# The first pair of w_ffn_in blocks as plain products instead of Strassen-type products

## The chip, the cores and the metric

The kernel runs on one core of one Trainium2 chip. The metric is the device time of one execution in microseconds (us). The kernel before has a median of 2129.55 us over 3 runs (2124.32 to 2131.04).

## The reference

An encoder of two layers works on 1024 tokens of width 1024. In each layer a mixer (a Fourier group, windowed attention, memory attention) is followed by a SwiGLU block, and both are normed on the way in and out:

```
x = x + RMSNorm_post(mixer(RMSNorm_pre(x)))
h = RMSNorm_pre_ffn(x)
gate, up = split(h @ w_ffn_in)            # 1024 x 1024 times 1024 x 5632
x = x + RMSNorm_post_ffn((silu(gate) * up) @ w_ffn_out)
```

The change lies in `h @ w_ffn_in`, in both layers, and there in the first 256 columns of gate and of up.

## The kernel before, in words

All matrix products are in float32r, a rounded form of float32, in three passes: each operand is split into a rounded high part (a cast on ScalarE, ACT, line 151) and the rest (a subtraction on VectorE, DVE, or on GpSimd, POOL, line 152), and high x high, high x low and low x high are summed in PSUM. TensorE (PE) does the products. The tile framework puts in the waits and orders each engine's instructions by its own schedule, in which the order of the code is the priority; so the order on an engine can differ from that of the code. Each engine then works through its instructions in order.

**The quads.** `w_ffn_in` is worked in 11 pairs, p = 0 to 10, each of a gate quad and an up quad (`Quad`, line 1067). A quad covers 256 columns, 1024 input channels and 1024 tokens as 2 x 2 blocks and needs seven products of half blocks instead of eight (a Strassen scheme). `ORDER` (line 1065) is 2, 4, 5, 1, 6, 7, 3. One product is 12 matmuls of 128 x 128 on 512 tokens, so a quad has 84. For a product, `weights` (line 1083) adds or subtracts two weight blocks where it needs a sum (five of seven; line 1093, DVE) and splits the result. `step` (line 1111) runs the product and combines the results with copies (line 1108, ACT) and sums on DVE and POOL (lines 1123 to 1139). `gate_out` (1142) takes Silu of the four gate blocks, `up_out` (1150) multiplies and writes seven sums of them to `actd` in DRAM, from where `ffn_out` takes them.

**The token blocks.** The right hand sides are made once per layer by `Blocks` (line 1016). `tile` (1024) transposes one tile of 128 tokens on PE (line 1032, eight transposes into two PSUM tiles `hTp`) and copies it raw to SBUF on ACT (1033). Raw blocks are named by token half and channel half: b11 and b21 for tokens 0 to 511, b12 and b22 for the others. `sum(i, c)` (1035) makes a quarter of the split right hand side of product i: 2 is b11, 5 is b22, 4, 1 and 6 are sums of two blocks (line 1050; the one of 6 on POOL), and 7 and 3 are b21 and b12 after `last` (1058) has changed them (1062 on POOL, 1063 on DVE). Products 2 and 4 need the first token half alone, the others need all eight tiles.

**The passage from mixer to w_ffn_in.** The loop `for i in range(NT + 4)` (line 1345) skews four steps: attention scores and values of tile i (with `out_prep`, which splits and squares the attention result), `out` of tile i-2 (the mixer's last products, `mo`, whose columns are combined at line 1007, then norm, residual and norm, lines 318, 325 and 281, 289), `tile` of i-4, and loads for tile i-1. From i = 8 on the block sums and the first products are put in between: blocks 2, then the gate quad's load, blocks 4 and its product 2 at i = 9, and at i = 10 the up quad's load and the rest of products 2 and 4. Blocks 5, 1 and 6 follow as their tiles come.

**Space.** SBUF is laid out by hand in two arenas with numbered places; small rings give out places in turn: `qws` for raw quad weights, `wcs` for split weights, `wsums` and `sums` for sums, `acts`, `silus` and `sns` for outputs. `HB` (line 1019) says where each split block lies. PSUM has four tags of two buffers each, `sc`, `pT`, `av` and `pd`.

Of the kernel before, what the change touches and what calls it, by code (L numbers as in the profile page):

```python
# [19 lines left out]
P = 128  # L20
# [48 lines left out]
def tile_encoder(ctx: ExitStack, tc: tile.TileContext, T, C, out):  # L69
# [58 lines left out]
    ems, es_ring, y1s = run(16, 4, 2), run(33, 5, 3), run(6, 2, 1)  # L128
    sqs, pms, xfs = run(16, 2, 2), run(20, 2, 2), Ring(16, 20, 24, 28, 32, 0)
    qws, sns, silus, acts = Ring(32, 0, 16, 20), Ring(36, 38, 40, 42, 32, 34), run(8, 5, 2), run(18, 7, 2)  # L130
    sums, wsums = run(8, 4, 2), Ring(4, 6)
    ras, rbs, bsums, xs_ = run(40, 3, 2), run(46, 6, 2), Ring(58, 32, 34), Ring(36, 24)

    zzs, dhs, tabs = run(112, 2, 4), run(64, 2, 4), run(72, 4, 2)
    mps, phs, yys = run(24, 2, 4), run(16, 3, 4), run(104, 2, 4)
    wcs, abs_ = Ring(112, 116, 96, 100, 48, 52, 56, 60), Ring(80)

    def sm(n, name="v"):
        if name not in smp:
# [876 lines left out]
    class Blocks:  # L1016


        HB = {2: (64, 72), 4: (80, 88), 5: (16, 24), 1: (0, 8), 6: (32, 40), 7: (None, None), 3: (None, 104)}

        def __init__(self):
            self.raw, self.b = {}, {}

        def tile(self, h, t):
            half, c = divmod(t, 4)
            for kg in range(2):
                if c == 0:
                    self.raw[half, kg] = big(4, 512, dt=F32)
                pt = ps([4, P], "hTp", "pT")
                for j in range(4):  # L1030
                    k = kg * 4 + j
                    nc.tensor.transpose(pt[:, j, :], h[:, k * P : (k + 1) * P], ident)
                nc.scalar.copy(self.raw[half, kg][:, :, c * P : c * P + P], pt)

        def sum(self, i, c, lo_eng=None):

            b11, b21 = self.raw[0, 0], self.raw[0, 1]
            if i not in (2, 4):
                b12, b22 = self.raw[1, 0], self.raw[1, 1]
            sl = slice(c * P, c * P + P)  # L1040
            if i not in self.b:
                self.b[i] = [big(4, 512) if k is None else at(k, 4, 512, dt=F32R) for k in self.HB[i]]
            if i == 2:
                s = b11[:, :, sl]
            if i == 5:
                s = b22[:, :, sl]
            if i in (1, 4, 6):
                s = sums(4, P)
                x, y, op = (b21, b11, ALU.subtract) if i == 4 else (b11, b22 if i == 1 else b12, ALU.add)
                (nc.gpsimd if i == 6 else nc.vector).tensor_tensor(out=s, in0=x[:, :, sl], in1=y[:, :, sl], op=op)  # L1050
            if i == 7:
                s = b21[:, :, sl]
            if i == 3:
                s = b12[:, :, sl]
            hi, lo = (b[:, :, sl] for b in self.b[i])
            split(hi, lo, s, lo_eng)

# [9 lines left out]
    class Quad:  # L1067
# [6 lines left out]
        def load(self):  # L1074
            self.raw = []
            for kg in range(2):
                r = qws(4, 2, P)
                nc.sync.dma_start(
                    r, self.w[kg * 512 : kg * 512 + 512, self.c0 : self.c0 + 256].rearrange("(k p) (j c) -> p k j c", p=P, c=P)
                )  # L1080
                self.raw.append(r)

        def weights(self, i):
            a11, a12 = (r[:, :, 0] for r in self.raw)
# [64 lines left out]

    def up_out(q, g, actd, p):  # L1150

        V, G = nc.vector, nc.gpsimd
        a = [acts(512) for _ in range(4)]
        for i, c in enumerate(q.out):
            (G if i in (0, 3) else V).tensor_tensor(out=a[i], in0=c, in1=g[i], op=ALU.mult)  # L1155
        a11, a21, a12, a22 = a

        def put(i, s):
            nc.sync.dma_start(actd[i - 1, p], s)

        put(3, a11)
        put(4, a22)
        for i, x, y, eng in ((1, a11, a22, G), (2, a21, a22, V), (5, a11, a12, G)):
            s = acts(512)
            eng.tensor_tensor(out=s, in0=x, in1=y, op=ALU.add)
            put(i, s)
        V.tensor_tensor(out=a21, in0=a11, in1=a21, op=ALU.subtract)
        put(6, a21)
        G.tensor_tensor(out=a12, in0=a12, in1=a22, op=ALU.subtract)
        put(7, a12)  # L1170
# [1 line left out]
    def quads(l, p, hb):  # L1172
        return [Quad(l, j * DFF + 2 * p * P, hb) for j in range(2)]

    def ffn_in(l, hb, actd, first):

        for p in range(NFF // 2):
            gq, uq = quads(l, p, hb) if p else first
            order = ORDER if p else ORDER[2:]
            for q in (gq, uq):  # L1180
                if p:
                    q.load()
                for i in order:
                    q.step(i)
                if q is gq:
                    g = gate_out(gq)
            up_out(uq, g, actd, p)
            if p == 0:
                qws.ks, wsums.ks = (44, 48, 52, 56), (4, 6, 0, 2)

# [132 lines left out]
    for l in range(DEPTH):  # L1323
        mix.zf(1, 2)
        mix.kvz_load()
        kvz = mix.skewed(mix.kvz, mix.kvz_turn, NT)
        weave(mix.fourier_units(), kvz[:8] + [mix.q_load] + kvz[8:])
        q = mix.skewed(mix.q, mix.q_turn, NT)
        for u in q[:4]:
            u()  # L1330
        mem.load()
        weave(mix.mem_units(), q[4:8] + [mix.fm_load] + q[8:])
        fm = mix.fm_units(pmd)
        weave(mix.att_units(0), fm[:6] + [mix.out_load] + fm[6:])
        mix.out_gains()
        xs = x_in if l == 0 else x2d
        hb = Blocks()
        hs = {}
        first = gq, uq = quads(l, 0, hb)
        qws.ks, wsums.ks = (32, 0, 16, 20), (4, 6)  # L1340
        for r in (qws, wsums, xfs, sns, silus, acts, sums, wcs):
            r.i = 0
        mix.values_32()
        att = mix.att_units(1)
        for i in range(NT + 4):
            if i < NT + SKEW:
                att[i]()
            if 2 <= i < NT + 2:
                hs[i - 2] = mix.out(i - 2, x1d[i - 2])
            if i >= 4:  # L1350
                hb.tile(hs.pop(i - 4), i - 4)
            if 1 <= i < NT + 1:
                mix.out_rows(i - 1, xs[i - 1], pmd[i - 1])
            if i == NT:
                for c in range(4):
                    hb.sum(2, c)
            if i == NT + 1:
                gq.load()
                for c in range(4):
                    hb.sum(4, c)  # L1360
                gq.step(2)
            if i == NT + 2:
                uq.load()
                gq.step(4)
                uq.step(2)
                uq.step(4)
            if i >= NT:
                for n in (5, 1):
                    hb.sum(n, i - NT)
            if i > NT:  # L1370
                for c in (i - NT - 1,) if i < NT + 3 else (2, 3):
                    hb.sum(6, c)
                    hb.last(c)
        for n in (7, 3):
            for c in range(4):
                hb.sum(n, c)
        ffn_in(l, hb, actd, first)

        junks.ks = (6,)
        nhT = [None, None]  # L1380
        st = {}
        if l + 1 < DEPTH:
            mem = Memory(l + 1, 16, 0, 16, 28, "pT")
            mix = Mix(l + 1, nhT, mem)

        xt = {}

        def last_x(t):
            xt[t] = xs_(D)
            nc.sync.dma_start(xt[t], x1d[t])  # L1390

        def last_tile(t, f):
            if t == 0:
# [12 lines left out]

        last = l + 1 == DEPTH
        abs_.i = 0
        abs_.ks = (64, 72, 80, 88, 16, 24, 0, 8, 32, 40, 48, 56, 96, 104, 112) if last else (80, 88, 48, 56, 96, 104)

        def after(i):
            if last:
                return
            if i == 5:
                mem.make()
            if i == 1:
                mix.zf_load()
# [49 lines left out]
```

## Time and profile before

The profile shows one execution of the kernel. In a row of a group, after the bar, stand busy us, mean ns of one, and the idle time before it with what ended it. A timeline row has start, length, engine, line, operation, names, count, and in brackets the idle time before it and what released it. A row of stretches gives for each engine busy time and, in brackets, the number of instructions.

| What | Value |
|---|---|
| Median of 3 runs | 2129.55 us |
| The profiled execution's own time | 2127.03 us |
| Its span, first to last instruction | 2125.2 us |
| PE busy with matmuls | 2008.2 us (94%) |
| DVE busy | 1594.6 us (75%) |
| ACT busy | 1068.3 us (50%) |
| POOL busy | 862.9 us (41%) |
| Mean granted TensorE clock | 0.974 |

### The profile page before, as it was taken

How to read it: one execution, taken by the hardware profiler on the slowest of the kernel's cores; microseconds unless marked ns; L12 is line 12 of the kernel's file. 1: busy time of each engine (PE TensorE's matmuls, PEld its weight loads, DVE VectorE, ACT ScalarE, POOL GpSimd, SP SyncE). 2: the span in 40 equal slices, each digit the busy share in tenths (PEclk: the TensorE clock that was granted, in tenths of full speed). 3: DMA queues.
4: the chain of work that ended last, by engine and by line, in shares of the span. 5: the costliest groups of instructions: out<-in, count | busy, mean ns of one | idle time of the engine just before them, and what ended most of it. 6: DMA issues, size and time to landing. Idle time of an engine off the chain costs nothing. (4 is left out here: it accounts for less than half of the span.)

```text
span 2125.2 us, 28513 instructions
## 1 busy us (share of the span) xinstructions
PE 2008.2 (94%) x9586; PEld 1655.2 (78%) x9586; DVE 1594.6 (75%) x2445; ACT 1068.3 (50%) x2269; POOL 862.9 (41%) x858
## 2 busy tenths in 40 slices
PE   7998999699999999999899979997999999989997
PEld 6886787488888887888778868775888888877885
DVE  7568666998877877667967686669887877877674
ACT  6477767553333334444545676775333333345441
POOL 4234437643423434321544444576443423432222
PEclk9999999899999999999999989998999999999998
DMA  6112122422332326987721122142332332389872
GB/s 222 45 50 65 65 95 106 152 65 95 122 100 94 111 95 193 352 270 263 257 84 45 49 70 99 67 143 95 104 109 95 119 100 93 119 290 328 278 229 79
DMA packets 173603, 287.52 MB, mean 135 GB/s; under 512 B 15480, under 2 KB 73360, under 8 KB 173456
## 3 DMA queue, kind: packets, MB, share of 16 engines
q1 hardware_dynamic: 165392, 266.82, 37.9%
q10 hardware_dynamic: 8064, 18.88, 2.3%
q8 instruction: 75, 1.23, 0.2%
q14 instruction: 72, 0.59, 0.1%
HBM read 219.06 MB, written 66.58 MB: 134 GB/s over the span
## 5 line engine op out<-in xcount | busy, mean ns | idle before, releaser
L151 ACT CAST arena_r<-arena_f 128x512 fp32r<-128x512 f32 (+1 forms) x780 | 444.6, 592 | 679.8 <-PE qz L1103 116.4
L152 DVE TENSOR_TENSOR arena_r<-arena_f,arena_r 128x512 fp32r<-128x512 f32 x676 | 545.2, 829 | 173.8 <-ACT arena_r L151 170.2
L1234 PE MATMUL fo<-arena_r 128*128 128x512 f32 x1848 | 437.5, 398 | 28.4 <-ACT arena_r L151 15.2
L1234 PEld LDWEIGHTS fo<-arena_r 128*128 128x128 f32 x1848 | 354.1, 193 | 106.9 <-ACT arena_r L151 17.8
L1103 PE MATMUL qy<-arena_r 128*128 128x512 f32 x1056 | 264.0, 399 | 27.8 <-ACT arena_r L151 22.9
L1103 PEld LDWEIGHTS qy<-arena_r 128*128 128x128 f32 x1056 | 202.7, 193 | 73.6 <-ACT arena_r L151 24.0
L1093 DVE TENSOR_TENSOR arena_f<-arena_f 128x512 f32<-128x512 f32 x220 | 204.6, 933 | 5.1
L1103 PE MATMUL qz<-arena_r 128*128 128x512 f32 x704 | 196.0, 389 | 0.2 <-DVE arena_r L152 0.2
L1123 POOL TENSOR_TENSOR arena_f<-arena_f 128x512 f32<-128x512 f32 x44 | 73.1, 1660 | 294.5 <-ACT arena_f L1108 294.5
L1215 POOL TENSOR_TENSOR arena_f<-arena_f 128x512 f32<-128x512 f32 x50 | 72.5, 1454 | 229.4 <-DMA arena_f<-in_w_ffn_out 145.0
L1103 PEld LDWEIGHTS qz<-arena_r 128*128 128x128 f32 x704 | 132.0, 188 | 28.0 <-DVE arena_r L152 0.7
L1155 POOL TENSOR_TENSOR arena_f<-arena_f 128x512 f32<-128x512 f32 x44 | 73.5, 1672 | 173.4 <-DVE arena_f L1135 126.3
L152 POOL TENSOR_TENSOR arena_r<-arena_f,arena_r 128x256 fp32r<-128x256 f32 (+2 forms) x104 | 84.1, 813 | 126.9 <-ACT arena_r L151 95.0
L1103 PE MATMUL qw<-arena_r 128*128 128x512 f32 x528 | 127.6, 389 | 0.8 <-ACT arena_r L151 0.8
L1103 PE MATMUL qx<-arena_r 128*128 128x512 f32 x528 | 127.7, 389 | 0.5 <-ACT arena_r L151 0.5
L1103 PE MATMUL qx<-big,arena_r 128*128 128x512 f32 x528 | 127.0, 389 | 0.0
L1103 PEld LDWEIGHTS qw<-arena_r 128*128 128x128 f32 x528 | 99.1, 188 | 21.8 <-ACT arena_r L151 1.2
L1103 PEld LDWEIGHTS qx<-arena_r 128*128 128x128 f32 x528 | 99.1, 188 | 21.4 <-ACT arena_r L151 0.9
L1103 PE MATMUL qz<-big,arena_r 128*128 128x512 f32 x352 | 115.5, 389 | 0.0
L1103 PEld LDWEIGHTS qx<-big,arena_r 128*128 128x128 f32 x528 | 99.1, 188 | 20.5
L162 PE MATMUL mo<-arena_r 128*128 128x512 f32 x384 | 102.2, 403 | 3.2 <-DVE arena_f L1007 3.2
L162 PE MATMUL mo<-big,arena_r 128*128 128x512 f32 x384 | 102.9, 407 | 0.3 <-ACT arena_f L967 0.3
(225 smaller groups left out, 3570.6 us busy)
## 6 DMA issues: line engine op xcount, KB each, us to landing
arena_f<-in_w_ffn_out SPq DMA_DIRECT2D x264, 256.0 KB, 4.3
arena_f<-in_w_ffn_in SPq DMA_DIRECT2D x88, 512.0 KB, 3.6
actd<-arena_f SPq DMA_DIRECT2D x154, 256.0 KB, 3.7
arena_f<-actd SPq DMA_DIRECT2D x154, 256.0 KB, 4.1
arena_f<-in_w_in SPq DMA_DIRECT2D x40, 256.0 KB, 2.7
arena_f<-in_x SPq DMA_DIRECT2D x16, 512.0 KB, 5.0
arena_f<-in_w_out SPq DMA_DIRECT2D x32, 256.0 KB, 2.7
pmd<-arena_f ACTq DMA_DIRECT2D x32, 256.0 KB, 2.0
```

The lines of the kernel that those rows point to most:

```text
L151: nc.scalar.copy(hi, src)
L152: return (lo_eng or nc.vector).tensor_tensor(out=lo, in0=src, in1=f32(hi), op=ALU.subtract)
L162: mm(self.dst, a, b, start=self.i == 0, stop=self.i == self.n - 1)
L1093: nc.vector.tensor_tensor(out=s, in0=a, in1=b, op=op)
L1103: mm(pt, a, b, start=start and n == 0, stop=n == 11, skip_group_check=not start)
L1123: nc.gpsimd.tensor_tensor(out=self.v, in0=self.v, in1=self.s2, op=ALU.add)
L1155: (G if i in (0, 3) else V).tensor_tensor(out=a[i], in0=c, in1=g[i], op=ALU.mult)
L1215: (nc.vector, nc.gpsimd)[k % 2].tensor_tensor(out=s, in0=x, in1=y, op=op)
L1234: mm(pt, ab[:, 0, x, sl], ab[:, 1, y], start=new and first and j == 0, stop=last and j == 2, skip_group_check=not new)
```

## The change

For p = 0 the two quads are no longer done by seven products but by eight products of plain blocks: `plain(half)` computes the two 128-column results of one token half with 48 matmuls, so a quad takes 96. `plain_half` runs both quads for one half, applies Silu to the gate results straight from PSUM and multiplies the up results with them straight from PSUM. The first half is written at i = 9, after tile 5, and the second after the loop. `act_sums` is the end of the former `up_out`.

The plain blocks are split straight from the PSUM tile of the transposes, by a cast, a subtraction and the raw copy; plain blocks (0,0) and (1,1) then serve as blocks 2 and 5. Blocks 4, 1, 6, 7 and 3 are made after the loop, 4 ahead of the second half and the others behind it. The weights of p = 0 are split whole (`plain_weights`), without sums; both quads' loads come at i = 8. Several places and rings are renumbered; block 1 now lies where plain block (0,1) was, block 6 where (1,0) was, and `sums` shares places 4 and 6 with `wsums`.

```diff
-    sums, wsums = run(8, 4, 2), Ring(4, 6)
+    sums, wsums = Ring(4), Ring(4, 6)
...
-    wcs, abs_ = Ring(112, 116, 96, 100, 48, 52, 56, 60), Ring(80)
+    wcs, abs_ = Ring(16, 20, 24, 28, 48, 52, 56, 60), Ring(80)
...
-        HB = {2: (64, 72), 4: (80, 88), 5: (16, 24), 1: (0, 8), 6: (32, 40), 7: (None, None), 3: (None, 104)}
+        PLAIN = {(0, 0): (64, 72), (0, 1): (80, 112), (1, 0): (88, 96), (1, 1): (0, 8)}
+        HB = {4: (32, 40), 1: (80, 112), 6: (88, 96), 7: (None, None), 3: (None, 104)}
...
-                nc.scalar.copy(self.raw[half, kg][:, :, c * P : c * P + P], pt)
+                split(*(b[:, :, sl] for b in self.plain[key]), pt)
+                nc.scalar.copy(self.raw[key][:, :, sl], pt)
+            self.b[2], self.b[5] = self.plain[0, 0], self.plain.get((1, 1))
...
+        def plain_weights(self, k0):
+
+            self.w = []
+            for kg in range(2):
+                hi, lo = (at(k0 + 8 * kg + 4 * i, 4, 2, P, dt=F32R) for i in range(2))
+                split(hi, lo, self.raw[kg])
+                self.w.append((hi, lo))
+
+        def plain(self, half):
+
+            res = []
+            for j in range(2):
+                pt = ps([512], "qp", ("sc", "av")[j])
+                acc = Acc(pt, NK)
+                for kg in range(2):
+                    (wh, wl), (bh, bl) = self.w[kg], self.hb.plain[half, kg]
+                    for k in range(4):
+                        acc.add(wh[:, k, j], wl[:, k, j], bh[:, k], bl[:, k])
+                res.append(pt)
+            return res
...
+    def plain_half(first, half, g, a):
+
+        for q in first:
+            for j, pt in enumerate(q.plain(half)):
+                if q is first[0]:
+                    g[j, half] = silus(512)
+                    nc.scalar.activation(g[j, half], pt, AF.Silu)
+                else:
+                    a[j, half] = acts(512)
+                    nc.vector.tensor_tensor(out=a[j, half], in0=pt, in1=g[j, half], op=ALU.mult)
...
-        qws.ks, wsums.ks = (32, 0, 16, 20), (4, 6)
+        qws.ks, wsums.ks, sums.ks, acts.ks = (8, 12, 40, 44), (4, 6, 0, 2), (4, 6, 32, 34), (36, 38, 18, 20, 22, 24, 26)
...
             if i == NT:
-                for c in range(4):
-                    hb.sum(2, c)
+                gq.load()
+                uq.load()
+                gq.plain_weights(16)
             if i == NT + 1:
-                gq.load()
-                for c in range(4):
-                    hb.sum(4, c)
-                gq.step(2)
-            if i == NT + 2:
-                uq.load()
-                gq.step(4)
-                uq.step(2)
-                uq.step(4)
-            if i >= NT:
-                for n in (5, 1):
-                    hb.sum(n, i - NT)
-            if i > NT:
-                for c in (i - NT - 1,) if i < NT + 3 else (2, 3):
-                    hb.sum(6, c)
-                    hb.last(c)
+                uq.plain_weights(48)
+                plain_half(first, 0, g0, a0)
+        for c in range(4):
+            hb.sum(4, c)
+        plain_half(first, 1, g0, a0)
+        act_sums([a0[k] for k in ((0, 0), (0, 1), (1, 0), (1, 1))], actd, 0)
+        for n in (1, 6):
+            for c in range(4):
+                hb.sum(n, c)
+        for c in range(4):
+            hb.last(c)
         for n in (7, 3):
             for c in range(4):
                 hb.sum(n, c)
-        ffn_in(l, hb, actd, first)
+        qws.ks, qws.i, acts.ks, acts.i = (48, 52, 56, 44), 0, (18, 20, 22, 24, 26, 28, 30), 0
+        ffn_in(l, hb, actd)
...
-        abs_.ks = (64, 72, 80, 88, 16, 24, 0, 8, 32, 40, 48, 56, 96, 104, 112) if last else (80, 88, 48, 56, 96, 104)
+        abs_.ks = (64, 72, 32, 40, 0, 8, 80, 112, 88, 96, 104, 16, 24, 48, 56) if last else (80, 88, 48, 56, 96, 104)
```

More of the change, by code (lines that the diff above doesn't have):

```diff
@@ L1016, in tile_encoder @@
     class Blocks:
-        HB = {2: (64, 72), 4: (80, 88), 5: (16, 24), 1: (0, 8), 6: (32, 40), 7: (None, None), 3: (None, 104)}
+        PLAIN = {(0, 0): (64, 72), (0, 1): (80, 112), (1, 0): (88, 96), (1, 1): (0, 8)}
+        HB = {4: (32, 40), 1: (80, 112), 6: (88, 96), 7: (None, None), 3: (None, 104)}
         def __init__(self):
-            self.raw, self.b = {}, {}
+            self.raw, self.plain, self.b = {}, {}, {}
         def tile(self, h, t):
             half, c = divmod(t, 4)
+            sl = slice(c * P, c * P + P)
             for kg in range(2):
+                key = half, kg
                 if c == 0:
-                    self.raw[half, kg] = big(4, 512, dt=F32)
+                    self.raw[key] = big(4, 512, dt=F32)
+                    self.plain[key] = [at(k, 4, 512, dt=F32R) for k in self.PLAIN[key]]
                 pt = ps([4, P], "hTp", "pT")
@@ L1032, in tile @@
                     nc.tensor.transpose(pt[:, j, :], h[:, k * P : (k + 1) * P], ident)
-                nc.scalar.copy(self.raw[half, kg][:, :, c * P : c * P + P], pt)
+                split(*(b[:, :, sl] for b in self.plain[key]), pt)
+                nc.scalar.copy(self.raw[key][:, :, sl], pt)
+            self.b[2], self.b[5] = self.plain[0, 0], self.plain.get((1, 1))
         def sum(self, i, c, lo_eng=None):
-            b11, b21 = self.raw[0, 0], self.raw[0, 1]
-            if i not in (2, 4):
-                b12, b22 = self.raw[1, 0], self.raw[1, 1]
+            b11, b21, b12, b22 = (self.raw.get(k) for k in ((0, 0), (0, 1), (1, 0), (1, 1)))
             sl = slice(c * P, c * P + P)
@@ L1042, in sum @@
                 self.b[i] = [big(4, 512) if k is None else at(k, 4, 512, dt=F32R) for k in self.HB[i]]
[L1043 to L1046, printed above, removed]
             if i in (1, 4, 6):
@@ L1050, in sum @@
                 (nc.gpsimd if i == 6 else nc.vector).tensor_tensor(out=s, in0=x[:, :, sl], in1=y[:, :, sl], op=op)
[L1051 to L1054, printed above, removed]
+            else:
+                s = (b21 if i == 7 else b12)[:, :, sl]
             hi, lo = (b[:, :, sl] for b in self.b[i])
@@ L1150, in up_out, with act_sums @@
     def up_out(q, g, actd, p):
-        V, G = nc.vector, nc.gpsimd
         a = [acts(512) for _ in range(4)]
         for i, c in enumerate(q.out):
-            (G if i in (0, 3) else V).tensor_tensor(out=a[i], in0=c, in1=g[i], op=ALU.mult)
+            (nc.gpsimd if i in (0, 3) else nc.vector).tensor_tensor(out=a[i], in0=c, in1=g[i], op=ALU.mult)
+        act_sums(a, actd, p)
+    def act_sums(a, actd, p):
+        V, G = nc.vector, nc.gpsimd
         a11, a21, a12, a22 = a
@@ L1173, in quads, with ffn_in @@
         return [Quad(l, j * DFF + 2 * p * P, hb) for j in range(2)]
[L1175 to L1179, printed above, removed]
+    def plain_half(first, half, g, a):
[4 more added lines that the diff above has]
+                    nc.scalar.activation(g[j, half], pt, AF.Silu)
+                else:
+                    a[j, half] = acts(512)
+                    nc.vector.tensor_tensor(out=a[j, half], in0=pt, in1=g[j, half], op=ALU.mult)
+    def ffn_in(l, hb, actd):
+        for p in range(1, NFF // 2):
+            gq, uq = quads(l, p, hb)
             for q in (gq, uq):
-                if p:
-                    q.load()
-                for i in order:
+                q.load()
+                for i in ORDER:
                     q.step(i)
@@ L1187, in ffn_in @@
             up_out(uq, g, actd, p)
-            if p == 0:
-                qws.ks, wsums.ks = (44, 48, 52, 56), (4, 6, 0, 2)
     def out_sums(l, actd, i, k):
@@ L1344, in tile_encoder @@
         att = mix.att_units(1)
+        g0, a0 = {}, {}
         for i in range(NT + 4):
```

## The prediction

> **What bounds the kernel now.** I began with the page of the profile: span, engine shares and the slices over time.
>
> ```profile
> span 2125.2 us, 28513 instructions
> PE 2008.2 (94%) x9586; PEld 1655.2 (78%) x9586; DVE 1594.6 (75%) x2445; ACT 1068.3 (50%) x2269; POOL 862.9 (41%) x858
> ...
> PE   7998999699999999999899979997999999989997
> ```
>
> PE (TensorE) carries the kernel, so a matmul that is added costs its full time unless it lands where PE now stands still. Of the 40 slices (53.1 us each) the one with a 6 (372 to 425 us) and the 7 of 1435 to 1488 us lie where the mixer's last token tiles pass into `w_ffn_in`, which is where the change acts. So next I asked for the stretches of both layers: the attention part, and from the mixer's last matmul to the end of the first pair of quads.
>
> ```profile
> core 0: us, PE busy (x) PEld busy (x) DVE busy (x) ACT busy (x) POOL busy (x), PEclk, DMA share, GB/s
> 340.00:397.40 57.40, 54.32 (x321) 41.05 (x320) 45.49 (x68) 41.58 (x101) 44.08 (x53) 1.00 0.42 144
> 397.40:459.30 61.90, 45.46 (x185) 35.95 (x185) 58.85 (x78) 33.51 (x59) 26.32 (x18) 0.83 0.21 67
> ...
> 1438.60:1499.10 60.50, 46.93 (x185) 36.55 (x184) 55.69 (x77) 35.24 (x62) 32.31 (x17) 0.83 0.24 79
> ```
>
> Each pair stretch holds 168 quad matmuls and 16 transposes (185 PE instructions with a straggler), at a mean granted clock of 0.83. DVE is busy 58.85 of 61.90 us there: VectorE, not PE, sets the pace. PE's timeline in layer 0 shows how, with two full-speed products at the end for scale:
>
> ```profile
> 395.41 2.09 PE L162 MATMUL mo<-arena_r 128*128 128x512 f32 x8
> 406.38 1.22 PE L1103 MATMUL qy<-arena_r 128*128 128x512 f32 x2 [8.88 <-ACT arena_r L151]
> 409.21 4.50 PE L1103 MATMUL qy<-arena_r 128*128 128x512 f32 x10 [1.62 <-DVE arena_r L152]
> 413.55 1.03 PE L1032 MATMUL hTp<-const,arena_f 128*128 128x128 f32 x8
> ...
> 428.40 0.60 PE L1032 MATMUL hTp<-const,arena_f 128*128 128x128 f32 x4
> ...
> 432.13 2.88 PE L1103 MATMUL qw<-arena_r 128*128 128x512 f32 x12
> ...
> 486.61 2.88 PE L1103 MATMUL qy<-arena_r 128*128 128x512 f32 x12
> 489.33 2.88 PE L1103 MATMUL qw<-arena_r 128*128 128x512 f32 x12
> ```
>
> Starts 486.61 and 489.33 give 2.72 us per product of 12, so 0.227 us per matmul; eight transposes take 1.0. After 432 PE is dense. Before that it idles 8.88 and 1.62 us and once more, and ten matmuls took 4.50 us, 0.45 each, half rate. Only products 2 and 4 of both quads (48 matmuls) can run before tile 7 is transposed at 429.0. The waits of this stretch say what holds them:
>
> ```profile
> PE qy L1103 <- ACT arena_r L151: 14.5, 2, 8.9
> ACT arena_r L151 <- DVE arena_f L1093: 13.8, 7, 5.4
> ```
>
> PE waits for a cast of weights, and that cast for the weight sum of L1093, which stands in DVE's full queue.
>
> What the stretch loses in layer 0 is 61.9 - 168 x 0.227 - 2.0 = 21.8 us, in layer 1 60.5 - 38.1 - 2.0 = 20.4 us. That is all this change can get.
>
> **The change, part by part.** *More PE work.* Two plain quads are 2 x 96 = 192 matmuls in place of 168: 24 more, 5.4 us per layer, 10.9 in all, at no place hidden once PE is dense. *Earlier PE work.* 96 of the 192 need only tiles 0 to 3, twice what could run early before; after tile 7 there remain 96 (21.8 us) in place of the 120 that ran after 429 besides u4 (27.2 us plus 2.7). *Less on DVE and ACT in the stretch.* The rows for this:
>
> ```profile
> L152 DVE TENSOR_TENSOR arena_r<-arena_f,arena_r 128x512 fp32r<-128x512 f32 x672 | 543.5, 831 | 173.8 <-ACT arena_r L151 170.2 <-PE qz L1103 0.7 <-DMA arena_f<-in_w_ffn_out 0.7
> ...
> L1093 DVE TENSOR_TENSOR arena_f<-arena_f 128x512 f32<-128x512 f32 x220 | 204.6, 933 | 5.1
> ...
> L1138 DVE TENSOR_TENSOR arena_f<-qz,arena_f 128x512 f32<-128x512 f32 x44 | 30.4, 690 | 53.6 <-PE qz L1103 53.6
> ...
> L152 DVE TENSOR_TENSOR arena_r<-hTp,arena_r 128x512 fp32r<-128x512 f32 x32 | 21.7, 686 | 14.9 <-ACT arena_r L151 14.7
> ...
> L1050 POOL TENSOR_TENSOR arena_f<-big,big 128x512 f32<-128x512 f32 x8 | 15.1, 1893 | 23.5 <-ACT big L1033 13.2 <-DVE arena_r L152 10.3
> ...
> L151 ACT CAST arena_r<-hTp 128x512 fp32r<-128x512 f32 x32 | 18.5, 588 | 12.2 <-PE hTp L301 12.1
> ...
> L518 DVE TENSOR_TENSOR arena_f<-arena_f 128x1024 f32<-128x1024 f32 x12 | 14.1, 1223 | 9.1 <-ACT arena_f L513 9.0
> ```
>
> DVE loses 10 weight sums and 14 weight subtractions, 10 x 0.93 + 14 x 0.83 = 20.9 us, and 8 combinations of products, 5.5 us. It gains 4 subtractions of 1024 columns (nearest row L518, 4 x 1.22 = 4.9; above, two of 0.83, 6.6) and 4 gate products, 2.8. Block 4's sums move later (its new place is freed by the mixer's last matmul): some 3 more; the plain subtractions of tiles 6 and 7 stand for those of blocks 2 and 5. That is about 44 us of DVE in place of 58.85.
>
> What PE still loses has three terms.
> - *Start.* The second weight load of the gate quad reuses space that the last `out_prep` reads; on SP's queue the two loads of the up quad stand behind it, and their weights wait too. The rows:
>
> ```profile
> 393.99 1.18 POOL L152 TENSOR_TENSOR arena_r<-arena_f,arena_r 128x256 fp32r<-128x256 f32 x1
> arena_f<-in_w_ffn_in SPq DMA_DIRECT2D x88, 512.0 KB, 3.6
> ```
>
> 395.2 + 3.6 = 398.8, cast of two widths 1.2, subtraction 1.2: 401.2. The first 12 matmuls need only the earlier load and cover 397.5 to 400.2, so 1 us if DVE takes it at once; the bounds are 0 and today's 8.9; I take 3, since DVE's queue holds the chains of tiles 5 to 7. After a long gap PE restarted at half rate (0.45 each above); 12 such matmuls are 2.7 more, left to the upper bound. [...]
> - *Boundary.* If the transposes of tiles 6 and 7 are put behind the first half, their four PSUM tiles pass through two buffers, each held for cast, subtraction and copy, 0.59 + 0.69 + 0.59 = 1.9 us: up to 4.3. If they slip in between, 0. I take 2.
> - *Start of p=1.* Its first weight sum uses a ring slot (4) that block 6's sum also uses, and block 6 overwrites plain block (1,0), which PE reads until 12 matmuls (2.7 us) before the end. Cast 0.59, subtraction 0.83, sum 0.93, cast 0.59, subtraction 0.83 are 3.8, less 2.7: 1.1 at best, 5.4 if block 6's other casts and subtractions go first. I take 4, near the upper end: block 6 precedes the weights in the program, so that p=1's weight casts queue on ACT behind four casts that wait for PE.
>
> Together 9 us. Layer 0: 21.8 - 9 - 5.4 = 7.4 saved; layer 1: 20.4 - 9 - 5.4 = 6.0; 13.4 in all.
>
> *Against it, the attention part.* Each of six tiles there gets two casts (0.59) and two subtractions (0.69), 8.2 us of DVE on 45.49 of 57.40, while most early sums of blocks 2 and 4 leave. The transposes' PSUM is held longer, and PE (54.32 of 57.40) could stall: between -1 (the pool engine is freed of sums) and 8.2 us; I take 1.5 per layer, 3 in all.
>
> *At nothing:* the Silu table load comes earlier, on an ACT that is half idle (33.51 of 61.90); weights and output blocks of `ffn_out` get other places, block 1's being free three products (8.2 us) before the end; without that cover, 2 us per layer.
>
> Sum: -13.4 + 3.0 = -10.4. The profiled execution took 2127.03 us (span 2125.2 and 1.8 around it): 2116.6, stated as 2117. The median of the three runs, 2129.55, lies 2.5 above that execution; the range has room for that.
>
> **The rivals.** *Nearly full cover:* weights ready at 397.5, transposes in between, 3 us lost in place of 9 and nothing in attention: 42.2 - 10.9 - 6 = 25.3, so 2102. For it: ACT stands half idle, DVE drops by a quarter. Against: every chain crosses four in-order queues.
>
> *DVE stays the bound:* POOL's eight block sums, now spread over the stretch, all move behind tile 7, beside some 24 block operations of DVE. Rows, with POOL silent in the first and busy in the last two:
>
> ```profile
> 423.13 2.48 DVE L152 TENSOR_TENSOR arena_r<-arena_f,arena_r 128x512 fp32r<-128x512 f32 x4
> 468.31 3.47 DVE L152 TENSOR_TENSOR arena_r<-arena_f,arena_r 128x512 fp32r<-128x512 f32 x2
> 466.21 3.32 POOL L1165 TENSOR_TENSOR arena_f<-arena_f 128x512 f32<-128x512 f32 x2
> ```
>
> 0.62 each against 1.73. Eight POOL sums of up to 1.89 are 15 us; over them DVE loses 15 x (1 - 0.62/1.73) = 9.6 us, so 44 becomes 54, with 4 us of waits 58 in each stretch: -3.9 - 2.5 + 3, 2124. [...]
>
> *Slower:* the weight casts come as late as now. Start 8.9 + 2.7 at half rate, boundary 3, p=1 5: 19.6 lost, above the 16.4 (layer 0) and 15.0 (layer 1) from which the 24 extra matmuls lose: +3.2 + 4.6 + 3 = 10.8, 2138. For it: today's 8.88. Against: no weight sums are left ahead of these casts.
>
> *Not as written:* instructions here are seen in another order than the code's (qw ahead of qz at 432). Should the first half land behind tile 7, all 192 matmuls (43.5 us) follow 412 to 422: about +1 to +10 per layer, 2138.
>
> **How the numbers follow.** Forecast 0.52 (2110 to 2122), full cover 0.15, DVE-bound 0.17, slower 0.11, not as written 0.05. A measurement here tells about 0.3% (6.4 us) from no change. Faster: 0.48 + 0.15 = 0.63; within: 0.04 + 0.17 = 0.21; slower: 0.16. The range 2104 to 2129 leaves out the slow cases and the end of full cover.
>
> **What would show it.** In the new profile: 192 matmuls of a new line, half of them before tile 7's transposes; the stretch from the mixer's last matmul to p=1 down from 61.9 to about 54.5; clock there above 0.83; PE's gap after the last `mo` near 3 us, and a gap of 1 to 5 before p=1's first qy. I am wrong if PE still idles 9 us at the start, if a new gap beyond 5 us stands ahead of p=1, or if attention lengthens by over 3 us per layer.

## The result, and the profile after

The changed kernel has a median of 2133.76 us over 11 runs (2130.79 to 2137.55), the kernel before 2127.46 over 11 runs beside them (2124.32 to 2131.04). The ratio is 1.0029, 95% interval 1.002 to 1.0038: slower by 6.3 us, at the edge of the 0.3% that can be told from no change. The forecast was 2117, its range 2104 to 2129. The profiled execution of the changed kernel took 2134.76 us, with a span of 2133.0 us. Its page, the span, the engine shares and PE's slices:

```profile
span 2133.0 us, 28494 instructions
...
PE 2020.2 (95%) x9634; PEld 1656.5 (78%) x9634; DVE 1577.4 (74%) x2409; ACT 1065.0 (50%) x2253; POOL 837.2 (39%) x846
...
PE   5998999999999999899999989998999999999996
```

The two weak slices of the passages (6 and 7 before) are 9 and 8 now. But the first slice, which the change doesn't touch, fell from 7 to 5. The stretches of the changed kernel, attention part and then last `mo` to p=1 for each layer (columns as in the prediction):

```profile
345.30:420.40 75.10, 70.21 (x380) 51.91 (x378) 52.29 (x90) 52.77 (x122) 45.01 (x59) 0.98 0.37 127
420.40:461.70 41.30, 37.60 (x166) 30.40 (x165) 33.91 (x43) 21.23 (x39) 14.91 (x12) 0.96 0.23 77
1388.90:1460.60 71.70, 68.33 (x375) 50.47 (x375) 52.65 (x85) 51.06 (x120) 43.94 (x58) 1.00 0.39 133
1460.60:1506.60 46.00, 38.25 (x171) 30.85 (x170) 36.43 (x48) 22.37 (x41) 16.05 (x13) 0.93 0.21 69
```

Layer 0's stretch is 41.3 us where it was 61.9, at a clock of 0.96 for 0.83, but the attention part ahead of it, into which 44 of the new products have moved, is 75.1 where it was 57.4. PE's timeline shows the new products (`qp`, line 162) and what is left of the gaps:

```profile
417.81 2.56 PE L162 MATMUL mo<-arena_r 128*128 128x512 f32 x10
...
421.70 11.16 PE L162 MATMUL qp<-arena_r 128*128 128x512 f32 x48
...
438.85 4.22 PE L162 MATMUL qp<-arena_r 128*128 128x512 f32 x11 [2.60 <-DVE arena_r L152]
...
443.25 18.64 PE L162 MATMUL qp<-arena_r 128*128 128x512 f32 x81
461.73 0.62 PE L1122 MATMUL qx<-arena_r 128*128 128x512 f32 x2
```

Products follow the last `mo` without a gap, 2.60 us are waited for tile 7's split, and p=1 follows without a gap. To see where the time went I cut both spans at events that both kernels have (start of a first product or transpose on PE, from the timelines). Two versions from the experiments below stand beside them, e1 and e2:

| us, from ... to ... | before | changed | e1 | e2 |
|---|---|---|---|---|
| start to first K/V product, layer 0 | 65.9 | 74.8 | 67.2 | 75.2 |
| to first block transpose, layer 0 | 276.3 | 272.7 | 274.1 | 272.9 |
| to p=1, layer 0 (holds the change) | 117.1 | 114.1 | 108.5 | 122.9 |
| p=1 to 10, layer 0 | 380.9 | 380.9 | 380.7 | 381.3 |
| `ffn_out`, to first K/V product, layer 1 | 243.6 | 248.0 | 244.7 | 244.7 |
| to first block transpose, layer 1 | 300.3 | 300.6 | 299.1 | 292.3 |
| to p=1, layer 1 (holds the change) | 115.0 | 115.5 | 110.3 | 128.7 |
| p=1 to 10, layer 1 | 381.1 | 380.8 | 380.8 | 381.5 |
| rest | 245.0 | 245.6 | 248.2 | 245.7 |
| span | 2125.2 | 2133.0 | 2113.6 | 2145.2 |

From the first block transpose to p=1 the changed kernel is 3.0 us shorter in layer 0 and 0.5 longer in layer 1. But the first block transpose itself comes 3.6 us earlier after the first K/V product than before (272.7 us for 276.3). From the first K/V product to p=1 it is 6.6 us shorter in layer 0 (386.8 for 393.4) and 0.8 longer in layer 1 (416.1 for 415.3). The start, in which no line changed, costs 8.9 us more, and the first `ffn_out` 4.4.

Each column is one execution, and its parts spread. In the last `ffn_out` (the row "rest") PE has the same order of instructions in all sixteen profiles of this case, and the part takes 241 to 254 us. In the first `ffn_out` e1 and four other versions below (e3, e5, e11, e14) share one order on PE and take 244 to 248 us. So the 4.4 us there can't be told from that spread, while the 8.9 us of the start can: every version below with three buffers outside the passage starts at 65.9 to 68.1 us, every one with two at 74.6 to 76.2 (e8, with four, at 70.0). PE's timeline of the start, changed kernel:

```profile
36.27 0.60 PE L412 MATMUL mTp<-const,arena_f 128*128 128x128 f32 x4
...
39.69 1.03 PE L412 MATMUL mTp<-const,arena_f 128*128 128x128 f32 x8
45.87 0.72 PE L162 MATMUL kmp<-arena_r 128*128 128x256 f32 x2 [5.15 <-ACT arena_r L151]
48.09 5.21 PE L162 MATMUL kmp<-arena_r 128*128 128x256 f32 x24 [1.50 <-DVE arena_r L152]
```

and of the kernel before:

```profile
23.39 1.09 PE L412 MATMUL mTp<-const,arena_f 128*128 128x128 f32 x4 [4.49 <-DVE arena_f L289]
...
39.27 5.92 PE L162 MATMUL kmp<-arena_r 128*128 128x256 f32 x48
```

The memory rows' transposes (`mTp`) stood in PE's queue from 23.4 us; now they come from 36.3, so that the memory's key products (`kmp`) wait 5.15 and 1.50 us for the splits of them. The work is the same, its order isn't.

Two sentences ahead of the prediction need putting right, and both matter here. The order of the code says less about an engine's order than is stated there: in the start no line changed, and yet its transposes moved from 23.4 to 36.3 us; in e5 below a call moves from i = 9 to behind the loop, and the time moves by 1.5 us. So a change in one place can move instructions in another; how the order comes about, no run shows. And PSUM does not have two buffers for each tag. Two are declared, but the kernel before is built with three for `pT`, the changed kernel with two. The runs agree: with three declared (e1) PE's order is that of the kernel before up to layer 0's passage, and the start takes 67.2 us (65.9 before); with two outside the passage (e2) the kernel before takes 75.2 us for it (74.8 in the changed kernel). The kernel before has early products `qy` of that tag inside the mixer, where the transposes need it too, and the changed kernel has none; that the counts differ for this reason is not shown. (There are five SBUF blocks `big` in the kernel before, and four in the changed kernel. e1 has four as well, so this isn't what moved the start.) The tag serves the transposes of the start, of the attention, of the blocks and of the next layer's memory rows (inside `ffn_out`), the products `qy` of every quad and one of the four product tiles of `ffn_out`.

### The profile page after: what moved, and what is told of

It reads as the page before. It is cut to its first block, busy times and chain, and to the rows that moved or that the text cites. A ratio compares the mean times of both kernels' runs of the same rounds, so it can differ in the third digit from the quotient of the medians.

```text
span 2133.0 us, 28494 instructions
## 1 busy us (share of the span) xinstructions
PE 2020.2 (95%) x9634; PEld 1656.5 (78%) x9634; DVE 1577.4 (74%) x2409; ACT 1065.0 (50%) x2253; POOL 837.2 (39%) x846
## 5 line engine op out<-in xcount | busy, mean ns | idle before, releaser
L151 ACT CAST arena_r<-arena_f 128x512 fp32r<-128x512 f32 (+3 forms) x760 | 436.4, 595 | 679.5 <-PE qz L1122 116.2
L152 DVE TENSOR_TENSOR arena_r<-arena_f,arena_r 128x512 fp32r<-128x512 f32 (+2 forms) x656 | 537.6, 841 | 163.7 <-ACT arena_r L151 148.4
L1122 PE MATMUL qy<-arena_r 128*128 128x512 f32 x960 | 230.9, 389 | 0.0
L1122 PEld LDWEIGHTS qy<-arena_r 128*128 128x128 f32 x960 | 180.2, 188 | 37.4
L1112 DVE TENSOR_TENSOR arena_f<-arena_f 128x512 f32<-128x512 f32 x200 | 193.6, 969 | 12.1 <-DMA arena_f<-in_w_ffn_in 5.5
L1122 PE MATMUL qz<-arena_r 128*128 128x512 f32 x640 | 178.2, 389 | 0.0
L1142 POOL TENSOR_TENSOR arena_f<-arena_f 128x512 f32<-128x512 f32 x40 | 60.2, 1505 | 285.0 <-ACT arena_f L1127 285.0
L1244 POOL TENSOR_TENSOR arena_f<-arena_f 128x512 f32<-128x512 f32 x50 | 76.4, 1530 | 222.1 <-DVE arena_r L152 114.4
L1122 PEld LDWEIGHTS qz<-arena_r 128*128 128x128 f32 x640 | 120.1, 188 | 24.9
L1173 POOL TENSOR_TENSOR arena_f<-arena_f 128x512 f32<-128x512 f32 x40 | 66.4, 1660 | 162.2 <-DVE arena_f L1154 125.6
L1122 PE MATMUL qw<-arena_r 128*128 128x512 f32 x480 | 115.8, 389 | 0.0
L1122 PE MATMUL qx<-arena_r 128*128 128x512 f32 x480 | 115.6, 389 | 0.0
L162 PE MATMUL qp<-arena_r 128*128 128x512 f32 x384 | 96.4, 408 | 12.9 <-ACT arena_r L151 6.3
```

The lines of the kernel that those rows point to most:

```text
L151: nc.scalar.copy(hi, src)
L152: return (lo_eng or nc.vector).tensor_tensor(out=lo, in0=src, in1=f32(hi), op=ALU.subtract)
L162: mm(self.dst, a, b, start=self.i == 0, stop=self.i == self.n - 1)
L1112: nc.vector.tensor_tensor(out=s, in0=a, in1=b, op=op)
L1122: mm(pt, a, b, start=start and n == 0, stop=n == 11, skip_group_check=not start)
L1142: nc.gpsimd.tensor_tensor(out=self.v, in0=self.v, in1=self.s2, op=ALU.add)
```

## The experiments

Theory A: the lost third buffer cost the time, through the order, and the new products themselves gain what was forecast. Theory B: the new products and the longer attention part eat the gain. Ratios are to the kernel before, run beside each.

**e1: three buffers, nothing else.**

```
-PS_BUFS = {"sc": 2, "pT": 2, "av": 2, "pd": 2}
+PS_BUFS = {"sc": 2, "pT": 3, "av": 2, "pd": 2}
```

> The changed kernel with three PSUM buffers for the transposes' tag (pT) instead of two; nothing else. [...] Theory A (the lost third buffer, and not the new products, cost the time): the first K/V product comes at 66 us again (74.8 in the changed kernel, 65.9 before), the layer-0 ffn_out takes 243.6 again (248.0), the span is 2133.0 less 5.3 (what of the start's delay is still there at the first block transposes) less 4.4, 2123, and the ratio to before 0.997 to 0.9995. Theory B (the new products and the longer attention part eat the gain, and the start's delay is absorbed later): wherever the start lands, the span stays within 2.5 us of 2133.0, ratio 1.002 to 1.004.

Measured: 2113.36 us, ratio 0.9933 (0.992 to 0.9947). A held in its sign and went beyond its number: 14 us faster than before, 20 faster than the changed kernel. On PE the order is that of the kernel before until inside layer 0's passage. By the table the parts that hold the change are 8.6 and 4.7 us shorter than before, and 10.8 and 5.9 from the first K/V product (382.6 and 409.4 us). Its stretches, and PE's timeline behind the last `mo` of layer 0, which ends at 398.6:

```profile
339.10:398.60 59.50, 58.77 (x342) 44.28 (x342) 43.49 (x74) 44.36 (x105) 39.48 (x55) 1.00 0.44 147
398.60:449.75 51.15, 44.52 (x189) 35.48 (x188) 40.75 (x51) 25.05 (x44) 19.43 (x15) 0.90 0.22 72
1372.10:1434.40 62.30, 61.30 (x353) 46.29 (x353) 48.55 (x80) 46.66 (x116) 44.46 (x56) 1.00 0.42 144
1434.40:1484.60 50.20, 43.66 (x191) 35.10 (x190) 40.60 (x52) 25.59 (x45) 19.07 (x16) 0.93 0.22 74
```

```profile
406.12 10.28 PE L162 MATMUL qp<-arena_r 128*128 128x512 f32 x44 [0.49 <-DVE arena_r L152]
416.24 1.03 PE L1036 MATMUL hTp<-const,arena_f 128*128 128x128 f32 x8
417.79 0.66 PE L1036 MATMUL hTp<-const,arena_f 128*128 128x128 f32 x4 [0.52 <-DVE arena_f L1207]
419.12 0.97 PE L162 MATMUL qp<-arena_r 128*128 128x512 f32 x3 [0.68 <-ACT arena_r L151]
422.61 0.80 PE L162 MATMUL qp<-arena_r 128*128 128x512 f32 x1 [2.52 <-DVE arena_f L1207]
...
426.68 23.24 PE L162 MATMUL qp<-arena_r 128*128 128x512 f32 x92 [2.42 <-DVE arena_r L152]
449.75 1.52 PE L1122 MATMUL qx<-arena_r 128*128 128x512 f32 x6
```

**e2: the kernel before with two buffers outside the passage.** The transposes outside the loop and `w_ffn_in` get a tag `pS` of two, those inside keep three.

```
+        if tag == "pT" and outer[0]:
+            tag = "pS"
```

> The kernel before with two buffers for the transposes everywhere outside the passage from mixer to w_ffn_in, and three inside it (a tag of its own for the outside). Theory A: the start and ffn_out of layer 0 lose what the changed kernel lost there: first K/V product at 74.8 us, ffn_out of layer 0 248.0, span 2125.2 + 5.3 + 4.4 = 2134.9, ratio 1.003 to 1.006. Theory B: the order of the start changes, but the time is within 2.5 us of before, ratio 0.999 to 1.001.

Measured: 2146.38 us, ratio 1.0086 (1.0072 to 1.01). The start comes out as forecast (75.2 us), the first `ffn_out` does not (244.7 us, where A said 248.0). The loss is twice the number of A: besides the start, the way from the first K/V product to p=1 grew by 2.4 and 5.7 us (395.8 for 393.4, 421.0 for 415.3), though the passages keep three buffers; why isn't settled.

**e3, e4: the changed kernel with the third buffer only outside the passage, or only inside** (the same two tags).

> The changed kernel with three buffers for the transposes outside the passage and two inside it. Theory A, with the loss all outside the passage: as the kernel with three everywhere, 2123 of span, ratio 0.997 to 0.9995, and the passage as in the changed kernel (first block transposes to p=1: 114.1 and 115.5 us). If the third buffer also shortens the passage, this one is slower than three everywhere by that much. Theory B: within 2.5 us of 2133.0.

> The changed kernel with two buffers for the transposes outside the passage and three inside it. Theory A: start and ffn_out as in the changed kernel (74.8 us, 248.0), span 2133 less what the passage gains by a third buffer, 0 to 4 us: ratio 1.001 to 1.004. If the passage is what the third buffer is for: ratio 0.997 to 0.9995 here, and the outside version stays at 1.003.

Measured: e3 2129.96 us, ratio 1.0011 (1.0002 to 1.0021); e4 2126.55, ratio 0.9995 (0.9987 to 1.0004). The start follows the count outside (67.2 us in e3, 76.2 in e4). Neither alone gives the 20 us back: 4 outside, 7 inside, so that A's view of a loss all outside the passage falls. With two outside and three inside in both, the change takes 2146.4 (e2) to 2126.5 (e4), 20 us faster.

**e5: the first half written later.** On e1, the call for the first token half moves from i = 9 to behind the loop.

```
-                plain_half(first, 0, g0, a0)
...
+        plain_half(first, 0, g0, a0)
         for c in range(4):
             hb.sum(4, c)
```

> The changed kernel with three buffers for the transposes, and the first token half written after the loop, ahead of block 4's sums, instead of at i = 9. [...] Rival (the order of the code is the order of the engine, as this document says ahead of the prediction): the 73 products that now stand between the last mo and tile 7's transposes (398.8 to 416.2 us) move behind tile 7, 17 us per layer, 2147.

Measured: 2114.82 us, ratio 0.9941 (0.9929 to 0.9953), 1.5 us from e1, and not the rival's 2147: for this call the place in the code hardly counts.

**e6: plain blocks split from the raw copy.** On e1, instead of straight from PSUM.

```
-                split(*(b[:, :, sl] for b in self.plain[key]), pt)
                 nc.scalar.copy(self.raw[key][:, :, sl], pt)
+                split(*(b[:, :, sl] for b in self.plain[key]), self.raw[key][:, :, sl])
```

> The changed kernel with three buffers for the transposes, and the plain blocks split from the raw copy in SBUF instead of straight from PSUM: a transpose's buffer is free after one copy on ACT, and the cast and the subtraction come one copy (0.6 us) later. Theory A (the buffer is held long enough by cast, subtraction and copy that two are too few, but three are not): with three there is nothing to gain by freeing it earlier; 0.6 to 1.5 us more per layer at the wait for tile 7's split, and 24 DVE subtractions that read two SBUF inputs beside POOL: 2113 to 2119. Rival (the time the buffer is held still bounds the passage with three): 2105 to 2111.

Measured: 2133.4 us, ratio 1.003 (1.0019 to 1.0041). Both theories missed: 20 us slower than e1. The second half waits 9.16 us in layer 0 and 8.47 in layer 1. PE, DVE and POOL of e6:

```profile
435.07 23.45 PE L162 MATMUL qp<-arena_r 128*128 128x512 f32 x92 [9.16 <-DVE arena_r L152]
```

```profile
426.45 1.74 DVE L1050 TENSOR_TENSOR arena_f<-big,big 128x512 f32<-128x512 f32 x1
...
429.80 1.74 DVE L1061 TENSOR_TENSOR big<-big,big 128x512 f32<-128x512 f32 x1
431.47 1.75 DVE L152 TENSOR_TENSOR arena_r<-big,arena_r 128x512 fp32r<-128x512 f32 x1
...
434.34 0.68 DVE L152 TENSOR_TENSOR arena_r<-big,arena_r 128x512 fp32r<-128x512 f32 x1
```

```profile
429.29 3.37 POOL L1060 TENSOR_TENSOR big<-big,big 128x512 f32<-128x512 f32 x2
```

With the split taken from the raw block (`big`), the last blocks' subtractions stand in DVE's queue among the block sums (L1050, L1061), and each takes 1.75 us while POOL adds blocks, 0.68 when it stops. In e1 the same subtraction reads the transposes' tile. Its DVE and POOL:

```profile
424.75 1.87 DVE L152 TENSOR_TENSOR arena_r<-hTp,arena_r 128x512 fp32r<-128x512 f32 x3
```

```profile
424.24 2.95 POOL L1050 TENSOR_TENSOR arena_f<-big,big 128x512 f32<-128x512 f32 x2
```

Three subtractions from PSUM in 1.87 us, 0.62 each, with POOL busy beside them, and no block sum ahead of them.

**e7, e9: the gate weights behind the mixer's last product.** On e1, gate weights of p = 0 in places 32 to 47, block 4 in 16 and 24. In e7 they are split at i = 8 and so overwrite a part of `w_out` that tile 7 still needs; e9 splits them behind it.

```
-                gq.plain_weights(16)
             if i == NT + 1:
+                gq.plain_weights(32)
```

> The changed kernel with three buffers for the transposes, and the gate quad's split weights of p = 0 in places 32 to 47 (block 4 goes to 16 and 24, the small ring to 32 to 44), which the mixer's last products still read: the weights' casts can't begin before the mixer's last product, as in the kernel before. This prices the term start of the passage. Theory A: the first half begins 3 to 9 us after the last mo instead of 0.5 (before: 8.88 and 8.44 us), and the 10 to 20 products that are woven in ahead of it move behind it; tile 7's wait takes up part: 3 to 8 us per layer, 2119 to 2129. Rival (tile 7's norm and split alone set the end of the first half, the start is hidden): within 3 us of 2113.4.

> As the run before it with the gate quad's split weights in places 32 to 47, but with these weights split after the mixer's last products in the program's order as well (in the earlier run they stood ahead of tile 7's products and overwrote a part of w_out that these read). So the gate weights' casts and subtractions can't begin before the mixer's last product. Theory A (the start is a term of the passage, what the kernel before lost there): the first half begins 3 to 9 us after the last mo instead of 0.5 us, and the 9 to 20 products woven in ahead of it move behind: 3 to 8 us per layer, 2119 to 2129. Rival (tile 7's norm and split set when the second half begins, and the first half has slack before that): within 3 us of 2113.4.

Measured: e7 2119.84 us (ratio 0.9968, 0.9955 to 0.9981), e9 2119.77 (0.9965, 0.9954 to 0.9976). PE in e9, layer 0:

```profile
392.28 1.08 PE L162 MATMUL qp<-arena_r 128*128 128x512 f32 x4
...
397.16 21.15 PE L162 MATMUL qp<-arena_r 128*128 128x512 f32 x92 [3.36 <-DVE arena_r L152]
```

The times are A's lower end, and the gaps are there: 3.4 us here and 3.7 in layer 1. But the passages are not where the time is lost. From the last `mo` to p=1 it is 53.0 us in both layers, 2 and 3 more than in e1; yet no product stands ahead of the last `mo` any more, and from the first block transpose to p=1 e9 takes 104.2 and 111.3 us where e1 takes 108.5 and 110.3, so in sum 3 us less. What is longer in e9's profile is the first `ffn_out`, by 5.6 us, in another order on PE (block 4 and the small ring lie elsewhere). So the gaps are shown, and that they cost the 6 us isn't: the rival's slack fits the passages better.

**e8: four buffers** on the changed kernel.

> The changed kernel with four buffers for the transposes. Theory A (a third buffer was missing, and with three the transposes no longer wait for one): within 4 us of 2113.4. Rival (the time falls with each buffer, since the transposes are the bound of start, mixer and ffn_out): 2100 to 2108.

Measured: 2112.2 us, ratio 0.9928 (0.9913 to 0.9943), as e1 within the spread. Three are enough.

**e10: the split straight from PSUM alone**, in the kernel before, for its plain blocks 2 and 5.

```
+                i = {(0, 0): 2, (1, 1): 5}.get((half, kg))
+                if i:
...
+                    split(*(b[:, :, c * P : c * P + P] for b in self.b[i]), pt)
```

> One part of the change alone: the kernel before (three buffers, seven products per quad), with its two plain blocks 2 and 5 split straight from the transposes' PSUM tile instead of from the raw copy. Theory A (the direct split pays in the changed kernel because there tile 7's own subtraction is what the second half waits for; before, the start is bound by the weights' casts, 8.9 us, and its first products wait for block 2, not for tile 7): 2122 to 2128, ratio 0.998 to 1.000. Rival (the direct split itself is worth some 8 us per layer, whatever the products): 2108 to 2115, ratio 0.991 to 0.995.

Measured: 2134.12 us, ratio 1.0033 (1.0021 to 1.0045), slower, where A said the same and the rival faster. The gap at layer 0's start is 10.5 us (8.9 before), and the weights' cast still bounds it:

```profile
405.13 1.22 PE L1110 MATMUL qy<-arena_r 128*128 128x512 f32 x2 [10.55 <-ACT arena_r L151]
```

So the split straight from PSUM gains nothing by itself. That fits A's reason, that it pays where tile 7's own subtraction is waited for; why it costs 7 us here is open.

**e11: e6 without POOL's block sums.**

```
-            nc.gpsimd.tensor_tensor(out=b21, in0=b21, in1=b22, op=ALU.add)
```

and the same for block 6's sum.

> The version with plain blocks split from the raw copy (three buffers, 2133.4 us), with POOL's eight block sums per layer (block 6's sums and the change of b21) left out, so that products 6 and 7 of the later pairs get other right hand sides. In that version the second half waits 9.2 us in layer 0 and 8.5 in layer 1 for DVE's subtraction of tile 7's block, behind seven DVE operations of 1.74 us each (0.68 when POOL is idle). Theory A (they take 1.74 because POOL reads SBUF beside them): without POOL's sums they take 0.68, the waits fall by 5 to 7 us each, 2119 to 2124. Rival (only the length of DVE's queue counts): the waits stay, 2130 to 2135.

Measured: 2130.87 us, ratio 1.0018 (1.0009 to 1.0028). DVE and PE:

```profile
428.41 1.28 DVE L1114 TENSOR_TENSOR arena_f<-arena_f 128x512 f32<-128x512 f32 x2
...
432.02 0.68 DVE L1063 TENSOR_TENSOR big<-big,big 128x512 f32<-128x512 f32 x1
432.62 0.68 DVE L152 TENSOR_TENSOR arena_r<-big,arena_r 128x512 fp32r<-128x512 f32 x1
```

```profile
433.36 23.53 PE L162 MATMUL qp<-arena_r 128*128 128x512 f32 x92 [6.03 <-DVE arena_r L152]
```

The operations do take 0.64 to 0.68 us without POOL's sums, where e6 has 1.74 and 1.75 beside them. But the waits fall by 3.1 us (9.16 to 6.03) and, in layer 1, 3.7 (8.47 to 4.75), not by 5 to 7. The 5 to 7 came from seven operations of 1.74 us; e6 has four in each layer, 4 x (1.74 - 0.68) = 4.2 us, and two weight sums (L1114, 1.28 us together) now go first in DVE's queue. The time falls by only 2.5 us, for another reason. From the first block transpose to p=1 e11 is 4.5 and 6.0 us shorter than e6 (113.9 for 118.4, 110.8 for 116.8), but a new wait of 3.62 us stands in pair 1 of each layer:

```profile
474.33 0.50 PE L1124 MATMUL qz<-big,arena_r 128*128 128x512 f32 x1 [3.62 <-ACT arena_f L1129]
```

So 3.1 and 3.7 us of e6's waits went with POOL's sums; how the rest of its 20 us divides isn't shown.

**e12: POOL's block sums on DVE,** on e1.

> The changed kernel with three buffers, and POOL's eight block sums per layer moved to DVE. DVE gets 8 operations of 0.68 us more, and its operations beside them no longer take 1.7 to 1.9 instead of 0.68. Theory A (the sharing costs about as much as it saves, and the split straight from PSUM has already taken DVE's operations off the path): within 4 us of 2113.4. Rival (DVE bounds the end of the passage): 2104 to 2109 if the sharing costs more than the moved work, 2118 to 2124 if the moved work does.

Measured: 2113.47 us, ratio 0.9931 (0.9919 to 0.9943), as A: no difference to e1.

**e13, e14: a tag of two for the block transposes alone,** on the changed kernel; e14 also has three buffers outside the passage.

```
-                pt = ps([4, P], "hTp", "pT")
+                pt = ps([4, P], "hTp", "pB")
```

> The changed kernel with two buffers for the transposes, but the block transposes of the passage under a tag of their own with two more; all other transposes keep the tag of two. Theory A (inside the passage the block transposes, whose buffer is held by cast, subtraction and copy, and the attention's transposes of the probabilities take each other's places): as with three buffers inside and two outside, 2126.5, or faster, 2120 to 2129; the last mo of layer 0 comes 55 to 62 us after the first block transposes (72.5 in the changed kernel, 56.9 with three everywhere). Rival (the passage's loss comes from the late start and the order drawn from it): 2131 to 2136, and 70 or more.

> As the run before it, with three buffers for the transposes outside the passage, two for the attention's inside it, and two of their own for the block transposes. Theory A: no transpose lacks a place any more, and the time is that of three everywhere, 2109 to 2118. Rival: as three outside and two inside, 2127 to 2133.

Measured: e13 2131.22 us (ratio 1.002, 1.001 to 1.0031), the rival's number, though layer 0's last `mo` comes 62.9 us after the first block transpose and not 72.5; e14 2120.18 (0.997, 0.9959 to 0.998), between the two. In e14 layer 0 reaches p=1 at 448.4 us, as e1 (449.8), but layer 1 takes 418.1 from its first K/V product to p=1, against 409.4. So with three buffers outside, a tag of their own for the block transposes gives layer 0 its time back in these profiles (382.2 us from the first K/V product to p=1, 382.6 in e1, 386.5 in e3), but not layer 1. With two outside it gives it to neither: in e13 layer 0 takes 388.4 us, in the changed kernel 386.8. What the third buffer does in layer 1, and why outside and inside don't add up, stays open.

## Why the prediction was wrong

**The step that failed** is the sum, "-13.4 + 3.0 = -10.4". It holds terms of the passage alone and so puts everything outside it at nothing; for the start it gives no reason. And the term under "Against it, the attention part" ("The transposes' PSUM is held longer, and PE could stall: between -1 and 8.2 us; I take 1.5 per layer") looked at the right resource and took its size as given. The change itself altered the size, from three buffers to two, and this acts through the order of the whole program. The start, at nothing in the sum, took 8.9 us more (the 4.4 us of the first `ffn_out` are within the spread), and layer 1 from its first K/V product to p=1 0.8 us more where the prediction has 4.5 less; layer 0 came out near the forecast (6.6 less, forecast 5.9). Put back in e1, the one buffer gives 7.6 us at the start, 4.2 in layer 0 and 6.7 in layer 1, most of the 19.4 us between the two spans. That the count did it is shown; how it does it inside the passages, in layer 1 above all, stays open.

Inside layer 0's passage the attention part took 75.1 us for 57.4. There 44 products of the first half (10.0 us) go ahead of the last `mo`, and 3.6 us are mixer work that stood ahead of the first block transpose before; some 4 us more are lost. The rival "not as written" thought only of the first half's own place. With three buffers (e1) the time is close to the forecast, 2113.4 for 2117, in part by luck, as the terms below show. I had named a gap beyond 5 us ahead of p=1 and an attention part longer by over 3 us per layer as signs that I was wrong; only the second came.

**More PE work, earlier PE work.** Right. PE's busy time in the profile rose from 2008.2 to 2020.2 us, with 10.9 forecast for the matmuls. In e1 the whole first half stands ahead of tile 7's transposes, 23 of its 96 products even ahead of the last `mo` in layer 0 and 22 in layer 1.

**The stretch.** Forecast 54.5 us, measured in e1 51.15 and 50.2. By the prediction's own formula the loss is 51.15 - 169 x 0.227 - 2.0 = 10.8 us in layer 0 (169 products are left in the stretch) and 50.2 - 170 x 0.227 - 2.0 = 9.6 in layer 1, for 9 forecast. The sum was near by luck, its terms weren't:
- *Start:* taken at 3, measured 0.49. A gap of 3 is what e9 shows when the weights do come late.
- *Boundary:* taken at 2, measured 0.52 + 0.68 + 2.52 + 2.42 = 6.1 us in layer 0 (6.4 in layer 1). The reason was wrong too: the transposes don't queue for buffers. The 2.52 us ended with a gate multiplication (L1207) and the 2.42 with tile 7's subtraction. DVE's timeline in e1 shows why the multiplication was late:

```profile
421.26 0.69 DVE L1112 TENSOR_TENSOR arena_f<-arena_f 128x512 f32<-128x512 f32 x1 [3.53 <-DMA arena_f<-in_w_ffn_in]
421.87 0.68 DVE L1207 TENSOR_TENSOR arena_f<-qp,arena_f 128x512 f32<-128x512 f32 x1
```

A weight sum of p=1 (L1112) that waits 3.53 us for its load stands ahead of it in DVE's queue, and ahead of tile 7's subtraction too. The 92 products behind these gaps ran 2.3 us slow.
- *Start of p=1:* taken at 4, measured 0.

**Attention part.** Forecast +1.5 us per layer. In e1 it is 59.5 us for 57.4, and PE busy 58.77 for 54.32: the 23 early products (5.2 us) filled PE's gaps, so that without them it is 3.1 us shorter, a gain that the prediction had nowhere. (Both windows begin 2.2 us ahead of the first block transpose.) In all, layer 0: 10.75 off the stretch, 2.1 onto the attention part, -8.6 for -5.9 forecast. Layer 1: -4.7 for -4.5.

**The rival that DVE stays the bound** came true only in e6: without the split from PSUM the second half waits 9 us for DVE. The prediction counted this split only as casts and subtractions. With the eight products it is worth 20 us (e6). The rival **slower** named late weight casts. e9 has them, with gaps of 3.4 and 3.7 us, and its time is 6 us above e1's, of which the passages show nothing; the prediction had 21 between that case and its forecast.

## What to carry to other kernels

Where the buffer counts and the order of instructions in the built program are not those of the code, compare both in untouched parts before believing that a change lost; here one number gave 20 us. Cut both spans at common events first: a difference in a part that no line touched is such a sign, if it is larger than parts of the same order differ by from one profile to the next (here up to some 4 us, and more in the last part). Hold the count fixed on both sides when a change is to be judged by itself, and split straight from PSUM where the next product waits for that split and POOL adds blocks beside DVE (without it e6 is 20 us slower than e1), but not as a rule (by itself it costs 7 us in e10).

## What the runs showed of the hardware

In e1's layer 0 the PE clock dropped to half with no gap of 0.9 us before it. In stretches that end where the granted clock changes (columns as in the prediction):

```profile
417.51:420.92 3.41, 1.62 (x7) 0.91 (x7) 0.22 (x1) 1.56 (x4) 0.00 (x0) 1.00 0.66 206
420.92:431.15 10.23, 6.12 (x16) 4.58 (x17) 9.89 (x12) 3.36 (x6) 6.24 (x4) 0.50 0.09 34
431.15:449.70 18.55, 18.55 (x83) 15.37 (x82) 13.81 (x22) 10.19 (x20) 4.75 (x3) 1.00 0.00 0
```

It fell to 0.50 at 420.92 us, when the gap of 2.52 us had only begun; in the 3.41 us ahead of that PE had been busy for 1.62, with transposes and three products, and no gap had yet lasted 0.9 us. It came back at 431.15, 4.5 us after the products ran without a gap (from 426.68). So 92 products took 23.24 us, 2.3 more than the 20.9 at 0.227 each. In e9 a gap of 3.36 us in layer 0 left the clock at 1.00 (the 92 products behind it took 21.15 us), and behind one of 3.74 in layer 1 it was 0.50 for 3.4 us (22.52 for 92). What share of work keeps the clock up no run here measures.

The half rate that the prediction read from 0.45 us per matmul is in the clock too: in the kernel before it was 0.50 from 399.77 to 413.42 us. PE worked without a gap only from 409.21, so the clock was back 4.2 us after that.

In the changed kernel, with two buffers, the 16 block transposes of four tiles ran in one go in layer 1 (1.91 us), so here the count acts through the order, and not as a wait of each transpose. PE there:

```profile
1474.90 1.91 PE L1036 MATMUL hTp<-const,arena_f 128*128 128x128 f32 x16
1482.39 2.08 PE L162 MATMUL qp<-arena_r 128*128 128x512 f32 x4 [5.58 <-ACT arena_r L151]
```

The products behind them wait 5.58 us for ACT's cast.
